# Two experts at a time: the first half of a pair's combine moves ahead of the next pair's gather

## The chip, the core and the metric

The kernel runs on one core of a Trainium2 chip. The core has a matrix engine (TensorE; PE in the profile, PEld where it loads weights), VectorE (DVE), ScalarE (ACT), GpSimd (POOL) and SyncE (SP), which here issues the weight transfers. Each engine works through its own list of instructions in order and waits at semaphores for the others. Matrix products land in PSUM, which this kernel uses as eight banks of 128 x 512 floats. The metric is the device time of one execution in microseconds (us), as the median of several runs.

## The reference

Two transformer blocks on 256 tokens of width 1024, in float32. The change touches the last part of the second block alone: a mixture of 32 experts (4 groups of 8, two experts per token, each with a hidden width of 512):

```
y = jnp.zeros_like(h)
for g in range(G):
    hg = jnp.einsum('td,edf->tef', h, w_gate[g])
    hu = jnp.einsum('td,edf->tef', h, w_up[g])
    act = jax.nn.silu(hg) * hu * comb[:, g, :, None]
    y = y + jnp.einsum('tef,efd->td', act, w_down[g])
```

`comb` is zero for every expert that the router did not choose for a token. The result is h + y.

## The kernel before

Everything ahead of the experts takes the first 555 us. Then the 32 experts are worked through as 16 pairs, p = 0 to 15, in the loop of `moe`; `step` ties each piece of TensorE's work behind the piece before it, so the order in which the loop is written is TensorE's order. An expert gets 64 slots for tokens; a pair fills the 128 rows of the array. For pair p the pieces are:

- `select`: VectorE builds a one-hot matrix `Pm` (token to slot); it does so one pair ahead.
- `gate_up` (L1544): the gate product and the up product, each 1024 deep, in 64 matmuls of 512 columns; the two experts stand side by side in the array. Weights come from HBM in tiles of 1 MB, two tiles per half of a product.
- `activate`: ScalarE takes silu of the gate product (L1553), VectorE multiplies it with the up product and the routing weight (L1554) into `act`.
- `cols` / `gather` (L1501): the tokens of pair p + 1 are gathered by 32 small matmuls into four banks; ScalarE copies each bank into `xg` (L1503).
- `turn_act` (L1560): four transposes of `act`; ScalarE copies them into `aT` (L1562).
- `weigh` (L1513): two small matmuls for the routing weights of pair p + 1, and some short VectorE work from L1515 on.
- `down` (L1571): the down product of pair p, into two banks `py[0]` and `py[1]`, the two halves of the output's 1024 columns.
- `back` (L1529): transposes `Pm` into `PTm`, which takes slots back to tokens.
- `parts`: splits one bank of `py` into a rounded high part `yH` (ScalarE, L124) and the remainder `yL` (VectorE, L125).
- `combine(pair, n)` (L1601): takes half n of `py` back to the tokens by four matmuls (two with `yH`, two with `yL`); VectorE adds the two result banks to `acc` (L1604). If the half has not been split yet, `combine` calls `parts` itself.

A pair's combine is done while the next pair is worked on: in iteration p the loop runs `parts` and `combine` of pair p - 1. The last pair has no successor; it splits and combines its own halves within `down` (the function `halves`).

Weights: 12 tiles of 1 MB per pair. They go through 23 buffers used in turn, and SyncE issues a transfer when its buffer has been read (L1366; the last pair's down weights in eight transfers of 512 KB, L1359). Each transfer also waits until the one eight before it has landed.

Buffers that the change touches: `act`, `aT` and `yH` share two buffers in turn (tag "act"); `yL`, `xg` and `PTm` have one each. Banks are given out by the scheduler from the eight.

Of the kernel before, what the change touches and what calls it, by code (L numbers as in the profile page):

```python
# [103 lines left out]
class Builder:  # L104
# [1528 lines left out]
    def moe(self):  # L1633
        nc, tc, I, big, tmp, c = self.nc, self.tc, self.I, self.big, self.tmp, self.c
        h3 = self.h3
        fg = self.v("ffn_norm_g_2")
        self.hg = big.tile([128, KD, S], F32, name="hg", tag="acc")
        nc.vector.tensor_mul(self.hg, h3, fg[:, :, None].to_broadcast([128, KD, S]))
        self.route()
        acc = self.acc  # L1640
        self.moe_pools += ([(self.wpool, "w")] * NW + [(self.spool, "s")] * NS + [(self.npool, "n")] * NN +
                           [(self.keep, "xT")])
        self.prefetch(NW + NS + NN + 1)

        np_ = NE // 2
        pairs = {}

        def select(p):

            u = tmp.tile([128, 2, 2], F32, name="ug")  # L1650
            nc.vector.tensor_scalar_add(u, self.u, float(-128 * p - 1))
            P = tmp.tile([128, 2, 128], F32R, name="Pm")
            self.onehot(P, u, 128)
            pairs[p] = {"P": P}

        at = [None]

        def step(f, *a):

            with ExitStack() as st:  # L1660
                if at[0]:
                    st.enter_context(tc.issue_after(at[0].ins))
                at[0] = f(*a)

        def cols(p):
            pairs[p]["xg"], last = self.gather(pairs[p]["P"])
            return last

        out = self.out.rearrange("o (t p) d -> (o p) t d", p=128)

        def store(t, n):
            nc.sync.dma_start(out[:, t, 512 * n:512 * n + 512], acc[:, t, 512 * n:512 * n + 512])
        select(0)
        step(cols, 0)
        self.route_rest()
        for p in range(np_):
            q, last = pairs[p], p == np_ - 1
            load = lambda j, nm, hf: self.expert_w(2 * p + j, nm, hf)
            if not last:
                select(p + 1)  # L1680
            step(self.gate_up, q, load)
            if p == 0:
                step(self.weigh, q, 0)
            self.activate(q)
            if p:
                self.parts(pairs[p - 1], 0)
            if not last:
                step(cols, p + 1)
            if p:
                step(self.combine, pairs[p - 1], 0)  # L1690
            step(self.turn_act, q)
            if not last:
                step(self.weigh, pairs[p + 1], 2 * p + 2)
            if p:
                step(self.combine, pairs.pop(p - 1), 1)
            step(self.back, q)
            if last:
                def halves(n, i, mm):
                    at[0] = mm
                    if n and i == 0:  # L1700
                        step(self.combine, q, 0, store)
                    if i:
                        self.parts(q, n)
                step(self.down, q, load, halves)
                step(self.combine, q, 1, store)
            else:
                step(self.down, q, load)
        self.more_rounds(store)

    def more_rounds(self, store):  # L1710
# [50 lines left out]
```

## Time and profile before

| what | value |
|---|---|
| median of 3 runs | 1024.68 us (1023.98 to 1024.88) |
| the profiled execution | 1024.59 us |
| its span, first to last instruction | 1022.8 us |
| PE busy | 978.9 us, 96% of the span |
| DVE, ACT, POOL busy | 515.2, 368.8, 27.1 us |
| weight transfers of the experts (gate, up, down) | 64, 64 and 60 of 1024 KB, 8 of 512 KB |

All times below are microseconds from the start of the span. A matmul's end in the profile is modelled, and matmuls overlap: the next one starts before the one ahead of it ends. The time that a piece of TensorE's work costs is therefore read from start to start. In the chain of waits, each piece is put from the end of the one before it to its own end.

### The profile page before, as it was taken

The numbers are of one execution on the slowest core, as the hardware profiler recorded it, in microseconds if no ns is written. First come the engines' busy times: TensorE is split into PE (matmuls) and PEld (weight loads), VectorE is DVE, ScalarE is ACT, GpSimd is POOL, SyncE is SP. The second block draws the span as 40 slices with busy tenths as digits, with TensorE's granted clock in tenths as the row PEclk, the third lists the DMA queues.
The fourth block names the chain that finished last, engine by engine and source line by source line (L and its number), as shares of the span: only waits on it lengthen the run. The fifth ranks groups of instructions, "written<-read, shape, count | busy, mean of one in ns | idle before, by whom it ended". The sixth has DMA issues, their size and how long they took to land.

```text
span 1022.8 us, 16189 instructions
## 1 busy us (share of the span) xinstructions
PE 978.9 (96%) x6676; PEld 707.6 (69%) x6676; DVE 515.2 (50%) x1004; ACT 368.8 (36%) x652; POOL 27.1 (3%) x25
## 2 busy tenths in 40 slices
PE   6999999999999999999998999999999999999996
PEld 5899998999999999988995444443444444443442
DVE  4868999668866775649954122112222222112223
ACT  3555565637556453556654111110111111111110
POOL 1010000010000000230000000000000000000000
PEclk9999999999999999999999999999999999999999
DMA  9978887539955546264568999999999999999961
GB/s 315 341 282 283 284 288 279 180 124 336 327 185 180 200 163 228 69 209 137 170 241 324 369 424 420 423 421 419 425 419 424 417 425 419 421 423 420 424 251 43
DMA packets 113350, 310.20 MB, mean 303 GB/s; under 512 B 9554, under 2 KB 59128, under 8 KB 96888
## 3 DMA queue, kind: packets, MB, share of 16 engines
q1 hardware_dynamic: 113182, 309.09, 79.6%
q8 instruction: 54, 0.88, 0.3%
q14 instruction: 24, 0.20, 0.1%
q10 hardware_dynamic: 90, 0.03, 0.0%
HBM read 308.05 MB, written 1.05 MB: 302 GB/s over the span
## 4 chain that ended last, share of the span: by engine, by line
PE 92%; ACT 3%; DVE 2%; DMA 1%; issue 1%; POOL 0%; SPq 0%; DVEq 0%; ACTq 0%; POOLq 0%
PE bank L1544 21%; PE bank L129 13%; PE bank L130 13%; PE bank L131 13%; PE bank L1571 11%; PE bank L1501 6%; PE bank L1601 4%; ACT aT L1562 1%; PE g L129 1%; ACT yH L124 1%; PE g L130 1%; PE g L131 1%; PE bank L1560 1%; ACT wh L124 1%; PE bank L970 1%; PE bank L961 1%
## 5 line engine op out<-in xcount | busy, mean ns | idle before, releaser
L1544 PE MATMUL bank<-we,xg 128*64 128x512 f32 x1024 | 222.5, 592 | 0.0
L1544 PEld LDWEIGHTS bank<-we,xg 128*64 128x64 f32 x1024 | 73.5, 137 | 145.7 <-issue 144.4
L125 DVE TENSOR_TENSOR yL<-bank,yH 128x512 fp32r<-128x512 f32 x32 | 22.1, 692 | 193.5 <-ACT yH L124 193.5
L1571 PE MATMUL bank<-we,aT 128*64 128x512 f32 x512 | 113.6, 595 | 0.3 <-ACT aT L1562 0.3
L129 PE MATMUL bank<-fH,wh 128*128 128x256 f32 x352 | 100.1, 285 | 2.1 <-ACT fH L997 2.1
L130 PE MATMUL bank<-fL,wh 128*128 128x256 f32 x352 | 100.4, 285 | 0.0
L131 PE MATMUL bank<-fH,wl 128*128 128x256 f32 x352 | 100.2, 285 | 0.0
L1553 ACT ACTIVATE act<-bank 128x512 f32<-128x512 f32 x16 | 9.6, 597 | 237.7 <-PE bank L1544 237.7
L1571 PEld LDWEIGHTS bank<-we,aT 128*64 128x64 f32 x512 | 35.3, 137 | 65.3 <-issue 63.5
L1604 DVE TENSOR_TENSOR acc<-acc,bank 128x512 f32<-128x512 f32 x64 | 41.1, 683 | 61.4 <-PE bank L1601 61.3
L1503 ACT COPY xg<-bank 128x256 f32<-128x256 f32 x64 | 23.9, 373 | 129.7 <-PE bank L1501 129.7
L129 PEld LDWEIGHTS bank<-fH,wh 128*128 128x128 f32 x352 | 68.2, 194 | 2.5 <-ACT fH L997 2.5
L131 PEld LDWEIGHTS bank<-fH,wl 128*128 128x128 f32 x352 | 68.3, 194 | 0.0
L130 PEld LDWEIGHTS bank<-fL,wh 128*128 128x128 f32 x352 | 68.3, 194 | 0.0
L1501 PEld LDWEIGHTS bank<-Pm,hn 128*128 128x128 f32 x512 | 59.4, 195 | 11.5 <-issue 11.5
L1501 PE MATMUL bank<-Pm,hn 128*128 128x128 f32 x512 | 62.4, 281 | 0.0
L125 DVE TENSOR_TENSOR wl<-wup,wh 128x2048 fp32r<-128x2048 f32 x22 | 50.2, 2288 | 10.6 <-ACT wh L124 10.6
L1554 DVE SCALAR_TENSOR_TENSOR act<-bank,comb,act 128x512 f32<-128x512 f32 x16 | 12.0, 750 | 76.1 <-PE bank L1544 76.0
L130 PE MATMUL bank<-aL,wh 128*128 128x256 f32 x176 | 49.5, 283 | 0.0
L131 PE MATMUL bank<-aH,wl 128*128 128x256 f32 x176 | 49.5, 283 | 0.0
L129 PE MATMUL bank<-aH,wh 128*128 128x256 f32 x176 | 48.8, 283 | 0.0
L124 ACT CAST wh<-wup 128x2048 fp32r<-128x2048 f32 x22 | 41.8, 1902 | 14.0 <-PE bank L130 13.3
(449 smaller groups left out, 2136.9 us busy)
## 6 DMA issues: line engine op xcount, KB each, us to landing
we<-in_w_exp_gate SPq DMA_DIRECT2D x64, 1024.0 KB
we<-in_w_exp_up SPq DMA_DIRECT2D x64, 1024.0 KB
we<-in_w_exp_down SPq DMA_DIRECT2D x60, 1024.0 KB
wup<-in_w_up SPq DMA_DIRECT2D x22, 1024.0 KB
wa<-in_w_ada SPq DMA_DIRECT2D x16, 1024.0 KB
wdn<-in_w_down SPq DMA_DIRECT2D x11, 1024.0 KB
wa<-in_w_ada SPq DMA_DIRECT2D x16, 512.0 KB
wgt<-in_w_in SPq DMA_DIRECT2D x8, 1024.0 KB
```

Source lines behind the costliest of these rows:

```text
L124: self.hi = self.nc.scalar.copy(hi, raw)
L125: self.nc.vector.tensor_sub(lo, raw, hi)
L129: mm(o, lh, rh, start=start, stop=False, skip_group_check=True)
L130: mm(o, lh, rl, start=False, stop=False, skip_group_check=True)
L131: return mm(o, ll, rh, start=False, stop=stop, skip_group_check=True)
L1501: last = nc.tensor.matmul(b[:, i], self.hn[:, t, cc + i], P[:, t].bitcast(F32), start=(t == 0), stop=(t == 1), skip_group_check=True)
L1503: nc.scalar.copy(xg[:, cc:cc + 2], b)
L1544: last = mm(b[64 * j:64 * j + 64], pair["xg"][:, kk, 64 * j:64 * j + 64], w[j][:, k], start=(kk == 0), stop=(kk == 7), skip_group_check=True)
L1554: nc.vector.scalar_tensor_tensor(act, pu, pair["comb"], act, op0=OP.mult, op1=OP.mult)
L1571: return self.nc.tensor.matmul(py[n][64 * j:64 * j + 64], aT[:, ff, 64 * j:64 * j + 64], w, start=(ff == 0), stop=(ff == 3), skip_group_ch ...
L1601: last = nc.tensor.matmul(bs[t], PT[:, t], y, start=(i == 0), stop=(i == 1))
L1604: nc.vector.tensor_add(o, o, bs[t])
```

## The change

The first half of pair p - 1 (`py[0]`) is now split at the end of iteration p - 1, directly behind `down`, instead of behind `activate` in iteration p. Its `combine` runs directly behind the gate and up products of pair p, ahead of the gather instead of behind it. The second half (`py[1]`) is split right behind that combine, by a call of its own ahead of the gather, where before `combine(..., 1)` called it behind `turn_act` and `weigh`. Nothing is added to or taken from the computation; every instruction is there as often as before.

```diff
@@ -1683,11 +1683,10 @@
                 step(self.weigh, q, 0)
             self.activate(q)
             if p:
-                self.parts(pairs[p - 1], 0)
+                step(self.combine, pairs[p - 1], 0)
+                self.parts(pairs[p - 1], 1)
             if not last:
                 step(cols, p + 1)
-            if p:
-                step(self.combine, pairs[p - 1], 0)
             step(self.turn_act, q)
             if not last:
                 step(self.weigh, pairs[p + 1], 2 * p + 2)
@@ -1705,6 +1704,7 @@
                 step(self.combine, q, 1, store)
             else:
                 step(self.down, q, load)
+                self.parts(q, 0)
         self.more_rounds(store)
```

On TensorE, in one pair of the loop (lines that begin with - stand there before, + now):

```order
 L1571 MATMUL bank<-we,aT 64x512 x16
 L1544 MATMUL bank<-we,xg 64x512 x32
-L1501 MATMUL bank<-Pm,hn 128x128 x16
 L1601 MATMUL bank<-yH,PTm 128x512 x2
 L1601 MATMUL bank<-yL,PTm 128x512 x2
+L1501 MATMUL bank<-Pm,hn 128x128 x16
 L1560 MATMUL bank<-cst,act 128x128 x4
 L1513 MATMUL bank<-carry,Pm 128x6 x2
```

The gather and the first combine change places; the transposes of `act` and all behind them stay. (A float32 matmul is two in the profile, so 32 here is 64 there.)

On ScalarE, one pair of the kernel before, with buffer numbers (bank_6967 and bank_6968 are the two halves of one pair's down product):

```order
L1553 ACTIVATE act_7052<-bank_7002 128x512
L124 CAST yH_7055<-bank_6967 128x512
L1503 COPY xg_7059<-bank_7060 128x256
L1503 COPY xg_7059<-bank_7066 128x256
L1503 COPY xg_7059<-bank_7072 128x256
L1503 COPY xg_7059<-bank_7078 128x256
L1562 COPY aT_7097<-bank_7092 128x512
L124 CAST yH_7109<-bank_6968 128x512
```

and the same stretch now, for the pair after it (bank_7126 and bank_7127 are the two halves):

```order
L124 CAST yH_7152<-bank_7126 128x512
L1553 ACTIVATE act_7215<-bank_7165 128x512
L124 CAST yH_7226<-bank_7127 128x512
L1503 COPY xg_7230<-bank_7231 128x256
L1503 COPY xg_7230<-bank_7237 128x256
L1503 COPY xg_7230<-bank_7243 128x256
L1503 COPY xg_7230<-bank_7249 128x256
L1562 COPY aT_7101<-bank_7096 128x512
```

The split of the second half has moved from behind the copy of `aT` to ahead of the four copies of `xg`, and that of the first half from behind the silu to ahead of it. On VectorE the second `yL` (L125) moves with it: it stands directly behind the two adds of the first combine now, ahead of the short work of `weigh` (L1515 to L1518); before it stood behind that.

## Rows read from the trace of the kernel before

**Rows 1.** Chain of waits, three pairs and the end: start us, us, what.

```profile
643.69 13.73 PE bank L1544 x64
...
672.33 13.73 PE bank L1544 x64
...
987.29 13.73 PE bank L1544 x64
...
1011.76 1.89 PE bank L1571 x8
```

**Rows 2.** Timeline of TensorE: start us, us, engine line op out<-in xcount [idle before].

```profile
657.36 3.84 PE L1501 MATMUL bank<-Pm,hn 128*128 128x128 f32 x32
660.95 0.71 PE L1601 MATMUL bank<-yH,PTm 128*128 128x512 f32 x2
...
661.96 0.60 PE L1560 MATMUL bank<-cst,act 128*128 128x128 f32 x4
662.32 0.36 PE L1513 MATMUL bank<-carry,Pm 128*128 128x6 f32 x2
663.72 0.73 PE L1601 MATMUL bank<-yH,PTm 128*128 128x512 f32 x2 [1.04 <-ACT yH L124]
...
665.03 0.29 PE L1529 MATMUL bank<-identr,Pm 128*128 128x128 f32 x2
665.25 1.08 PE L1571 MATMUL bank<-we,aT 128*64 128x512 f32 x4
```

**Rows 3.** Groups by line, 574 to 1010 us: xcount | busy us, mean ns | idle.

```profile
L1513 PE MATMUL bank<-carry,Pm 128*128 128x6 f32 x32 | 5.8, 253 | 0.0
```

**Rows 4.** Waits of TensorE, 585 to 1010 us: total us, times, longest.

```profile
PE bank L1601 <- ACT yH L124: 15.8, 15, 1.2
```

**Rows 5.** Timeline of ScalarE in the same pair.

```profile
661.23 0.37 ACT L1503 COPY xg<-bank 128x256 f32<-128x256 f32 x1 [0.52 <-PE bank L1501]
662.60 0.59 ACT L1562 COPY aT<-bank 128x512 f32<-128x512 f32 x1 [0.99 <-PE bank L1560]
663.08 0.59 ACT L124 CAST yH<-bank 128x512 fp32r<-128x512 f32 x1
```

**Rows 6.** Timeline of VectorE in the same pair.

```profile
661.92 1.28 DVE L1604 TENSOR_TENSOR acc<-acc,bank 128x512 f32<-128x512 f32 x2 [3.67 <-PE bank L1601]
...
663.70 0.69 DVE L125 TENSOR_TENSOR yL<-bank,yH 128x512 fp32r<-128x512 f32 x1
```

**Rows 7.** Stretches: us, busy (x) by engine, PEclk, DMA share, GB/s.

```profile
574.00:985.00 411.00, 396.05 (x2084) 184.12 (x2084) 97.62 (x277) 53.03 (x117) 0.00 (x0) 1.00 1.02 421
985.00:991.00 6.00, 6.00 (x32) 2.00 (x30) 0.00 (x0) 0.00 (x0) 0.00 (x0) 1.00 0.51 184
```

**Rows 8.** Timeline of SyncE: the last issue of weights.

```profile
978.99 0.50 SPq L1359 DMA_DIRECT2D we<-in_w_exp_down  x1
```

**Rows 9.** Timeline of TensorE in the last pair.

```profile
1000.96 0.73 PE L1601 MATMUL bank<-yH,PTm 128*128 128x512 f32 x2
...
1003.75 0.73 PE L1601 MATMUL bank<-yH,PTm 128*128 128x512 f32 x2 [1.16 <-ACT yH L124]
...
1005.04 0.29 PE L1529 MATMUL bank<-identr,Pm 128*128 128x128 f32 x2
```

**Rows 10.** Waits of SyncE, 960 to 980 us.

```profile
SPq L1359 <- DMA we<-in_w_exp_up: 0.7, 1, 0.7
```

**Rows 11.** Timeline of VectorE in the last pair.

```profile
1001.95 1.28 DVE L1604 TENSOR_TENSOR acc<-acc,bank 128x512 f32<-128x512 f32 x2
```

**Rows 12.** Stretches, as in rows 7: two idle times and what followed.

```profile
230.00:233.00 3.00, 0.93 (x6) 0.50 (x5) 1.17 (x3) 1.82 (x5) 0.00 (x0) 1.00 0.38 68
233.00:236.00 3.00, 3.00 (x17) 3.00 (x17) 2.62 (x8) 0.99 (x3) 0.00 (x0) 0.56 1.01 396
...
438.00:441.00 3.00, 1.73 (x13) 1.44 (x12) 2.33 (x2) 2.62 (x5) 2.67 (x2) 1.00 0.03 4
441.00:444.00 3.00, 3.00 (x23) 2.78 (x22) 1.75 (x1) 0.00 (x0) 2.82 (x2) 1.00 0.95 287
```

## The prediction

> **What bounds the kernel now.** I read the page first (the table above), then the chain of waits, then the timeline of each engine through one pair, and last the stretches of the weight transfers. The chain shows the experts as one repeated pattern: the products of pair after pair start 28.64 us apart (643.69 to 672.33), and it stays on TensorE almost throughout [rows 1]. The timeline of TensorE shows the one hole in a pair: after the two small matmuls of `weigh` it sits idle for 1.04 us until ScalarE has split the second half of the previous pair [rows 2]. It is there 15 times and costs 15.8 us [rows 4]. ScalarE's timeline says why: that split (663.08) stands behind the fourth copy of `xg` and the copy of `aT`, and `aT` waits for the transposes [rows 5]. The data have been ready since the last `down`; only the order of the list holds them back.
>
> The second bound hides behind that. From 574 to 985 us the DMA engines are full, share 1.02, and move 421 GB/s [rows 7]. A pair's weights are 12 x 1.0486 = 12.58 MB, which at that rate take 29.9 us, 1.25 more than TensorE needs for a pair. TensorE does not wait, because it lives on tiles loaded ahead, and that stock shrinks with each pair. What TensorE gains can be kept only as long as it lasts.
>
> **The change part by part.**
>
> *The wait that goes.* `weigh` has two matmuls in 0.36 us, one lasts 0.253 [rows 2, 3], so they start 0.11 apart, and a piece that waits for nothing would start at 662.32 + 0.22 = 662.54. The combine began at 663.72: 1.18 late. When nothing holds it, a combine takes 1.01 us up to the next piece (660.95 to 661.96); the second one took 1.31 (663.72 to 665.03), since `yL` also came late: another 0.30 [rows 2]. Together 1.48 us a pair. Pairs 1 to 14 have this pattern: 14 x 1.48 = 20.7 us.
>
> *What is late next.* Behind the second combine and `back`, `down` needs `aT`. The transposes start at 661.96, `aT` is copied from 662.60 to 663.19 [rows 2, 5]; `down` would start at 665.25 - 1.48 = 663.77, 0.58 later. The fourth `xg` copy now ends just ahead: it starts 0.28 after the gather's successor (661.23 against 660.95) and takes 0.37, so it leaves ScalarE 0.65 after the start of the transposes, when `aT` could start at 0.64. That cover stays, but it is the thinnest.
>
> *ScalarE.* The second `yH` now stands ahead of the `xg` copies. It needs the buffer that the first combine's `yH` matmuls read, so it runs from about 0.7 to 1.3 us after that combine starts. The first `xg` bank is ready only at about 1.9 (1.01 for the combine, and a quarter of the gather's 3.59). No collision.
>
> *VectorE.* Behind the products it has `act` and then the two adds. In the last pair, where the combine already follows the products, they start 0.99 after the combine and take 1.28 [rows 9, 11], so they end at 2.27; then `yL` (0.69, [rows 6]), done at 3.0. The second combine would start at 1.01 + 3.59 (gather, 657.36 to 660.95) + 0.36 + 0.22 = 5.2 [rows 2]. It needs `yL` and, in the built program, the bank that the second add has just read. Cover 2.2 to 2.9 us.
>
> *Moved at no cost.* A combine starts as soon behind the products as a gather does: 1000.96 against an end of 987.29 + 13.73 = 1001.02 in the last pair, 657.36 against 657.42 in another [rows 1, 2, 9]. `xg` comes 1.0 us later, but is read only behind `down`. The first half's split now stands ahead of the next silu; 13.73 us of products hide it. If one of these covers were gone, each would cost up to its length, 0.6 to 1.0 us a pair.
>
> *The weights.* SyncE's issues hang on buffers that TensorE has read. They come free earlier, which at a share of 1.02 can't raise the rate. So the weights land when they did, and the question is how early they were. At 985 us there are 6 x 184 = 1.10 MB to come [rows 7]; four tiles (4.19 MB) follow the last up tile, so that tile is in at 985 - 3.09 / 0.421 = 977.7. The last weight issue, at 978.99, waited for the landing of an up tile [rows 8, 10]: 979.0, so 1.3 us of notice come on top. Its products were due in the last quarter of `gate_up`: 987.29 + 0.75 x 13.73 = 997.6 [rows 1]. Spare: 18.6 us. One pair earlier it is 18.6 + 1.25 = 19.9, and TensorE has gained 13 x 1.48 = 19.2 by then: no wait. In pair 15 the gain of 20.7 exceeds the spare: TensorE waits about 2.1 us for up tiles, and 18.6 remain. The last down tiles are in by 991 + 1.3 and would be used at 1011.76 - 19.2 = 992.6 [rows 1, 7]: just in time.
>
> *The last pair.* There is no gather in it to cover VectorE. The adds end at 1001.95 + 1.28 = 1003.23, `yL` 0.69 later at 1003.92; before, the `yL` matmuls started 0.73 behind 1003.75, at 1004.48 [rows 6, 9, 11]. Gain 0.6. From there on, nothing changes.
>
> **Sum**, against the profiled execution (1024.59, 0.09 under the median of the runs): 18.6 + 0.6 = 19.2, so 1005.4 us. Bounds of the unknown: the spare can be read from 18.6 to 19.9 (landing at 977.7 instead of 979.0); the gain per pair from 1.04 (the idle time alone) to 1.48.
>
> **Rivals.**
>
> 1. *TensorE stays the bound to the end.* If the spare is over 20.7, all of it is kept: 20.7 + 0.6, so 1003.3. For it: the landing is inferred, not seen. Against: both readings of the spare lie below 20.7.
> 2. *`aT` takes the place of the wait.* Its cover is 0.58; if it comes 1.0 us later than I read, 0.4 us a pair stay: 14 x 1.06 + 0.6 = 15.4, below the spare, so 1009.2. For it: two copies meet on ScalarE. Against: they only touch.
> 3. *The wait for weights drops TensorE's clock.* About 2 us of idle time around 231 us were followed by a stretch at a granted 0.56, near the lower level of 1.2 GHz; 1.27 us idle around 439 were followed by 1.00 [rows 12]. Three us at 0.56 lose 1.3. My 2.1 us of waiting fall in two or three pieces with products between. If they count as one: about 1007. The Trainium skill (TensorE: Matmul & The Clock Gate, "What's actually happening") says that the throttled clock is the default and that activity releases it; the rows agree with that. By it alone a starved TensorE pays twice.
> 4. *The transfers bind already and nothing is gained.* A stage that moves 12.58 MB a pair at 421 GB/s can't run at 27.2 us a pair; with no stock it would stay where it is: 1024.6. For it: a share of 1.02 all through. Against: TensorE has 18.6 us in hand at the tightest place. The Trainium skill (DMA: Bandwidth & Descriptors, "Where 436 GB/s comes from") speaks for it: it puts the ceiling at 435 GB/s, which would be an estimated 28.9 us a pair, above the 28.64 of the trace. The trace's 421 is below that ceiling, as the rule wants.
> 5. *Slower.* VectorE's adds now decide when the second combine gets its bank. They have 2.9 us to spare; from 2.9 us late TensorE waits, from 4.4 (2.9 + 1.48) the change loses, and each us more costs 14. One us past that is 1038 or so. For it: three VectorE pieces now follow each other there. Against: they would be done 3.0 us after the combine starts, and nothing else stands among them.
>
> That the change does not do what it says is excluded by the order of the built program, in which the pieces stand as told.
>
> **Chances.** Forecast 0.62; rival 1 0.12; rival 2 0.10; rival 3 0.08; rival 4 0.05; rival 5 0.03. The range 1003.0 to 1008.5 holds the forecast and rivals 1 and 3, 0.82. A measurement of this kernel can tell 0.2%, 2 us, from no change: faster 0.92, same 0.05, slower 0.03.
>
> **What will show it.** In the changed profile, the wait of the combine for `yH` should be gone from all pairs but the very end; the products should start about 27.16 us apart from pair 2 to pair 14; the second `yH` should run before the first `xg` copy; in pair 15, and only there, TensorE should wait for up tiles, 2 us in all; the transfers should end at 988 to 991 us as before, at 421 GB/s. A period of 27.6 or more would mean a new wait in the pair (rival 2); no wait for weights at 1003, rival 1; a wait for weights in many pairs, that I read the stock too large.

## The result, and the profile after

| kernel | median us (range, runs) | profiled execution | its span |
|---|---|---|---|
| before | 1024.33 (1023.89 to 1024.88, 4) | 1024.59 | 1022.8 |
| after | 1007.44 (1005.38 to 1008.01, 4) | 1005.38 | 1003.5 |

The ratio is 0.9831, with an interval of 0.9814 to 0.9848: faster by 1.5 to 1.9%. Two repeats of the same kernel (`again` and `after_beside` below) had 1005.92 and 1006.34 us; the mean of its 14 runs is 1006.5. The forecast was 1005.4, its range 1003.0 to 1008.5.

The chain of waits first (start us, us, what). It answers to [rows 1]:

```profile
639.30 13.73 PE bank L1544 x64
...
666.46 13.73 PE bank L1544 x64
...
957.86 20.98 DMA we<-in_w_exp_up
978.88 3.65 PE bank L1544 x14
...
992.69 1.89 PE bank L1571 x8
```

The products of two pairs start 27.16 us apart instead of 28.64. Near the end, a transfer has entered the chain, which had only TensorE there before. The waits of TensorE from 555 to 1010 us (total us, times, longest), against [rows 4]:

```profile
PE bank L1544 <- DMA we<-in_w_exp_up: 2.2, 2, 1.4
PE bank L1601 <- DVE yL L125: 0.8, 1, 0.8
PE bank L1601 <- ACT yH L124: 0.7, 1, 0.7
PE bank L1571 <- ACT aT L1562: 0.3, 1, 0.3
```

The 15 waits for `yH` are gone; the one left stands at the end of the last pair, at 995 us, where before had one too (at 1014, outside the window of [rows 4]). New is a wait for up tiles. TensorE's timeline through one pair shows what stands where the wait was, against [rows 2]:

```profile
652.97 0.73 PE L1601 MATMUL bank<-yH,PTm 128*128 128x512 f32 x2
653.53 0.63 PE L1601 MATMUL bank<-yL,PTm 128*128 128x512 f32 x2
654.00 3.73 PE L1501 MATMUL bank<-Pm,hn 128*128 128x128 f32 x32
657.57 0.60 PE L1560 MATMUL bank<-cst,act 128*128 128x128 f32 x4
657.92 0.36 PE L1513 MATMUL bank<-carry,Pm 128*128 128x6 f32 x2
658.15 0.72 PE L1601 MATMUL bank<-yH,PTm 128*128 128x512 f32 x2
...
659.16 0.28 PE L1529 MATMUL bank<-identr,Pm 128*128 128x128 f32 x2
659.38 7.09 PE L1571 MATMUL bank<-we,aT 128*64 128x512 f32 x32
```

The second combine starts 0.23 us behind `weigh` and takes 1.01; nothing stands idle. ScalarE in the same pair, against [rows 5]:

```profile
653.73 0.59 ACT L124 CAST yH<-bank 128x512 fp32r<-128x512 f32 x1 [6.83 <-PE bank L1601]
655.09 0.37 ACT L1503 COPY xg<-bank 128x256 f32<-128x256 f32 x1 [0.77 <-PE bank L1501]
...
657.77 0.37 ACT L1503 COPY xg<-bank 128x256 f32<-128x256 f32 x1 [0.52 <-PE bank L1501]
658.20 0.59 ACT L1562 COPY aT<-bank 128x512 f32<-128x512 f32 x1
```

The split runs ahead of the four copies. `aT` is ready at 658.79, and `down` starts at 659.38: the thin cover of 0.6 us held. VectorE, against [rows 6]:

```profile
653.18 0.75 DVE L1554 SCALAR_TENSOR_TENSOR act<-bank,comb,act 128x512 f32<-128x512 f32 x1 [14.24 <-PE bank L1544]
653.97 1.28 DVE L1604 TENSOR_TENSOR acc<-acc,bank 128x512 f32<-128x512 f32 x2
655.17 0.68 DVE L125 TENSOR_TENSOR yL<-bank,yH 128x512 fp32r<-128x512 f32 x1
```

It is done at 655.85, 2.3 us before the second combine needs it. The last pair, on TensorE, is where the rest went (against [rows 9]):

```profile
965.13 7.89 PE L1544 MATMUL bank<-we,xg 128*64 128x512 f32 x34
973.86 3.65 PE L1544 MATMUL bank<-we,xg 128*64 128x512 f32 x16 [0.84 <-DMA we<-in_w_exp_up]
978.88 3.65 PE L1544 MATMUL bank<-we,xg 128*64 128x512 f32 x14 [1.37 <-DMA we<-in_w_exp_up]
982.46 0.73 PE L1601 MATMUL bank<-yH,PTm 128*128 128x512 f32 x2
...
985.41 0.73 PE L1601 MATMUL bank<-yL,PTm 128*128 128x512 f32 x2 [0.80 <-DVE yL L125]
...
986.19 5.37 PE L1571 MATMUL bank<-we,aT 128*64 128x512 f32 x24
...
992.62 1.94 PE L1571 MATMUL bank<-we,aT 128*64 128x512 f32 x8
```

Its products take 982.46 - 965.13 = 17.33 us. A pair that waits for nothing takes 13.84 (652.97 less the 639.13 at which this timeline starts that pair). So the weights cost 3.5 us, not the 2.2 that the waits show as idle. Matmul ends are modelled, so the beginning of a gap counts as busy. And around the gaps matmuls of the two experts, which otherwise start 0.01 us apart, run one by one: the last one ahead of the first gap starts alone at 972.42, the last two of the products at 981.51 and 981.94. The last row shows the end of it: the last `down` tiles are used at 992.62, and nothing waits for them.

The transfers run as before (stretches, columns as in [rows 7]):

```profile
574.00:985.00 411.00, 408.06 (x2155) 190.65 (x2154) 101.43 (x276) 58.26 (x121) 0.00 (x0) 1.00 1.02 420
```

One part of the difference between the two profiled executions is not the change's. The first products start at 560.3 us in the profile of before and at 558.8 in that of after. The same two stretches as in [rows 12], in after:

```profile
230.00:233.00 3.00, 0.93 (x7) 0.57 (x5) 1.36 (x3) 1.80 (x4) 0.00 (x0) 1.00 0.46 104
233.00:236.00 3.00, 3.00 (x26) 3.00 (x26) 2.73 (x8) 0.98 (x3) 0.00 (x0) 1.00 1.04 397
```

The idle time at 231 us is the same, but it was not followed by a stretch at 0.56. Ahead of it before was already 0.3 us behind, from the first 25 us; the stretch cost the other 1.1. So from here on runs are also compared by their *expert stage*: from the first of the products to the end of the span. It is 1022.8 - 560.3 = 462.5 us before and 1003.5 - 558.8 = 444.7 after.

The stage has a scatter of its own. VectorE's last add is followed only by the last store of `out`, and from that add to the end of the span it is 5.7 us in this trace of after, 6.3 and 6.5 in its two repeats, 6.0 before. So a difference of less than 0.8 us between two stages says nothing, and the sharper measure is *to the last add*: from the first product to the end of VectorE's last add. Its rows on VectorE, before and after:

```profile
1015.57 1.28 DVE L1604 TENSOR_TENSOR acc<-acc,bank 128x512 f32<-128x512 f32 x2 [0.59 <-PE bank L1601]
```

```profile
996.50 1.28 DVE L1604 TENSOR_TENSOR acc<-acc,bank 128x512 f32<-128x512 f32 x2 [0.59 <-PE bank L1601]
```

That is 456.6 us before (1015.57 + 1.28 - 560.27) and 439.0 after (996.50 + 1.28 - 558.82); the two repeats have 438.9 both. Of the 19.2 us between the profiled executions 17.6 are the change's, 1.4 the clock's ahead of the experts and 0.2 the last store's.

### The profile page after: what moved, and what is told of

It is laid out like the page before. It is cut to its first block, busy times and chain, and to the rows that moved or that the text cites. A ratio compares the mean times of both kernels' runs of the same rounds, so it can differ in the third digit from the quotient of the medians.

```text
span 1003.5 us, 16244 instructions
## 1 busy us (share of the span) xinstructions
PE 972.0 (97%) x6676; PEld 707.6 (71%) x6676; DVE 516.6 (51%) x1004; ACT 371.7 (37%) x652; POOL 27.1 (3%) x25
## 4 chain that ended last, share of the span: by engine, by line
PE 89%; DMA 3%; DVE 3%; ACT 2%; issue 1%; SPq 1%; POOL 0%; DVEq 0%; ACTq 0%; POOLq 0%
PE bank L1544 21%; PE bank L129 13%; PE bank L131 13%; PE bank L130 13%; PE bank L1571 11%; PE bank L1501 6%; PE bank L1601 3%; DMA we<-in_w_exp_up 2%; ACT wh L124 1%; DVE wl L125 1%; DMA wa<-in_w_ada 1%; PE g L130 1%; PE g L131 1%; PE bank L970 1%; PE bank L961 1%
## 5 line engine op out<-in xcount | busy, mean ns | idle before, releaser
L124 ACT CAST yH<-bank 128x512 fp32r<-128x512 f32 x32 | 18.7, 586 | 204.6 <-PE bank L1601 105.7
L1501 PE MATMUL bank<-Pm,hn 128*128 128x128 f32 x512 | 60.2, 276 | 0.0
L125 DVE TENSOR_TENSOR wl<-wup,wh 128x2048 fp32r<-128x2048 f32 x22 | 50.3, 2289 | 10.6 <-ACT wh L124 10.6
L125 DVE TENSOR_TENSOR yL<-bank,yH 128x512 fp32r<-128x512 f32 x32 | 22.0, 688 | 56.6 <-ACT yH L124 56.6
L129 PE MATMUL bank<-xH,wh 128*128 128x256 f32 x160 | 45.9, 290 | 0.6 <-ACT xH L1122 0.6
```

The costliest lines, as they stand in the source:

```text
L124: self.hi = self.nc.scalar.copy(hi, raw)
L125: self.nc.vector.tensor_sub(lo, raw, hi)
L129: mm(o, lh, rh, start=start, stop=False, skip_group_check=True)
L1501: last = nc.tensor.matmul(b[:, i], self.hn[:, t, cc + i], P[:, t].bitcast(F32), start=(t == 0), stop=(t == 1), skip_group_check=True)
```

## The experiments

Three questions: is the second half's split the whole gain; does the stock of weights cap it; and where does the capped part go. Each ratio is against the kernel before, run beside: 1024.48 us for `again` to `one_buffer_less`, 1024.82 for `second_split_late` to `fill_the_wait`, 1024.31 for the last two.

**The kernel after, again** (no edit).

> The changed kernel once more, as the base of this group. Theory 1 (the weights cap the gain): 1007.4 us as a median; TensorE waits about 2 us for up tiles in pair 15 and for nothing else in pairs 2 to 14, products 27.17 us apart. Theory 2 (no cap, the 2 us short of the forecast are spread between runs): the same time, but the wait for up tiles comes and goes. Clock: runs in which the clock falls at about 233 us, as in the profile of the kernel before, should be 1.4 us longer than runs in which it does not, whatever the experts do.

1005.92 us (1005.52 to 1006.89), ratio 0.9819 (0.9806 to 0.9833). That is 1.5 us under the 1007.4 that I expected. The wait for up tiles is 2.1 us (2.1 in `after_beside` too), so it does not come and go. The stage is 1004.1 - 558.8 = 445.3, to the last add 438.9. The first result holds.

**Fewer weights, after.** Eight tiles fewer to bring: for the second half of their down product eight experts use the tile loaded just before, so the output differs.

```diff
+            if nm == "down" and hf and e % 2 and 8 <= e < 24:
+                self.enext += 1
+                self.eloaded[key] = self.elast
+                continue
...
-            self.eloaded[key] = w
+            self.eloaded[key] = self.elast = w
```

> The changed kernel with 8 of the 192 weight tiles not loaded: in pairs 4 to 11 the second expert's second half of the down product uses the first expert's tile, so the output differs. The weights then land 8 x 2.49 = 20 us earlier at the end. Theory 1: the 2.2 us of waiting for up tiles in pair 15 go, so 2.2 us faster than the changed kernel as it is, about 1005.2 as a median. Theory 2: no difference.

1003.76 us (1002.82 to 1004.46), ratio 0.9797 (0.9784 to 0.9811). No wait for weights is left. TensorE's timeline in the last pair:

```profile
966.73 13.90 PE L1548 MATMUL bank<-we,xg 128*64 128x512 f32 x64
980.56 0.73 PE L1605 MATMUL bank<-yH,PTm 128*128 128x512 f32 x2
```

The products take 13.83 us again, 3.5 less than after. By the median it gains 2.2 us over `again`, as expected; but the first products of this execution came 1.6 us later than those of `again`, so the median hides a part. By the stage (1001.6 - 560.4 = 441.2) it is 4.1, of which 0.6 is the last store; to the last add, 438.9 - 435.5 = 3.4. The cap is real, and without it the change would be worth 456.6 - 435.5 = 21.1 us.

**Fewer weights, before.** The same edit on the kernel before.

> The kernel before with the same 8 tiles not loaded. Both theories: TensorE never waited for weights there, so 1024.3 us, no change. Together with the run before it this gives what the change is worth where weights are no limit: theory 1 says 14 x 1.47 + 0.5 = 21.1 minus nothing, so about 19.1 to 21.1 us.

1024.97 us, ratio 1.0003 (0.9994 to 1.0012), with the old wait still there (view of waits, 585 to 1010 us):

```profile
PE bank L1605 <- ACT yH L124: 15.8, 15, 1.2
```

To the last add it is 456.6 us, as before. So weights cost nothing there: the same bytes are a bound only once TensorE is faster.

**One buffer less, after.**

```diff
-        self.moe_pools += (... + [(self.npool, "n")] * NN + [(self.keep, "xT")])
-        self.prefetch(NW + NS + NN + 1)
+        self.moe_pools += (... + [(self.npool, "n")] * NN)
+        self.prefetch(NW + NS + NN)
```

> The changed kernel with 22 weight buffers in place of 23 (the last of the list is left out), nothing else. Theory 1: the transfers stop for full buffers around 561 us one tile earlier, so every later tile lands 2.49 us later, and the wait for up tiles in pair 15 (or one before it) grows from 2.2 to 4.7 us: 2.5 us slower than the changed kernel, about 1009.9. Theory 2: no difference, since 22 buffers still run far ahead of TensorE.

1009.97 us (1009.2 to 1010.22), ratio 0.9855 (0.984 to 0.987): 4.05 over `again` where 2.5 was expected. The stage is 1008.5 - 560.2 = 448.3, 3.0 over `again` (3.0 to the last add, too); the first products came 1.3 us later than those of `again`. The waits:

```profile
PE bank L1544 <- DMA we<-in_w_exp_up: 3.7, 3, 1.3
...
PE bank L1544 <- DMA we<-in_w_exp_gate: 0.2, 1, 0.2
```

A tile of 1.0486 MB is 2.5 us at 421 GB/s, and that less in stock costs 3.0. The wait now reaches back into pair 14.

**Second split late.** The kernel after without one line:

```diff
                 step(self.combine, pairs[p - 1], 0)
-                self.parts(pairs[p - 1], 1)
```

> The kernel after without its line that issues the second split beside the gather: the second combine again splits its own half, behind the ScalarE copy of aT, as before; the first combine stays ahead of the gather. Theory 1 (the gain is the wait for the second half's yH, which the early second split takes away): the wait of about 1.2 us for yH is back in front of the second combine in all 15 pairs, the period of a pair is 28.6 us again, the time 1024 us (1022.5 to 1025.5). Theory 2 (a part of the gain comes from the first combine's place directly behind the up products): period 27.4 to 28.3 us, time 1008 to 1019 us.

1024.61 us (1022.1 to 1025.16), ratio 0.9997 (0.9988 to 1.0007). The wait is back as it was (view of waits):

```profile
PE bank L1601 <- ACT yH L124: 15.8, 15, 1.2
```

Products start 28.62 us apart (642.86 to 671.48 in the chain). In this kernel the whole gain hangs on this line; moving the first combine alone gains nothing.

**Only the splits moved.** The kernel before with both splits ahead of the gather, in buffers of their own, and one weight buffer less; TensorE's order stays.

```diff
-NW, NM, NS, NT, NR, NX, NN = 3, 2, 4, 2, 7, 5, 3
+NW, NM, NS, NT, NR, NX, NN = 3, 2, 4, 2, 7, 5, 2
...
-        yH = self.tmp.tile([128, 512], F32R, name="yH", tag="act")
-        yL = self.tmp.tile([128, 512], F32R, name="yL", bufs=1)
+        yH = self.tmp.tile([128, 512], F32R, name="yH", tag="yH")
+        yL = self.tmp.tile([128, 512], F32R, name="yL")
...
             if p:
                 self.parts(pairs[p - 1], 0)
+                self.parts(pairs[p - 1], 1)
             if not last:
                 step(cols, p + 1)
```

> TensorE's order of the kernel before (gather, then both combines), but both splits issued ahead of the gather, in buffers of their own (two for yH, two for yL), paid for with one weight buffer less (22 instead of 23). Theory 1 (what counts is that the second split is ready, not where the first combine stands): no wait for yH or yL in front of the second combine, period about 27.2 us, time as the run with one buffer less: 1010 us (1008 to 1012.5). Theory 2 (the first combine has to cover the split's time): a wait of 0.5 us or more in each pair stays, in front of either combine or of the down products, period 27.7 us or more, time 1015 to 1024 us.

1008.2 us (1007.92 to 1009.11), ratio 0.9838 (0.9823 to 0.9853). TensorE's timeline in a pair:

```profile
654.60 3.84 PE L1501 MATMUL bank<-Pm,hn 128*128 128x128 f32 x32
658.19 0.71 PE L1601 MATMUL bank<-yH,PTm 128*128 128x512 f32 x2
...
659.56 0.36 PE L1513 MATMUL bank<-carry,Pm 128*128 128x6 f32 x2
659.78 0.72 PE L1601 MATMUL bank<-yH,PTm 128*128 128x512 f32 x2
...
661.02 7.09 PE L1571 MATMUL bank<-we,aT 128*64 128x512 f32 x32
```

No hole, 27.17 us a pair (640.94 to 668.11 in the chain). So the first combine need not stand ahead of the gather as such. What its place buys in the change is memory: the second `yH` takes over the buffer that the first combine has just read. Here the buffers of the splits were paid for with a weight buffer (whether there is room without that was not tried), and the time is near that of the run with one buffer less. It is 1.4 us better by the stage (446.9 against 448.3), 1.5 to the last add. Of this 1.1 are the last pair's, from the first combine to `down` (2.62 us against 3.73): the wait for `yL` is gone there.

**First split late.**

```diff
+                self.parts(pairs[p - 1], 0)
                 step(self.combine, pairs[p - 1], 0)
...
-                self.parts(q, 0)
```

> The kernel after, but the first half's split is issued behind the next pair's activation, directly ahead of the first combine, not at the end of its own pair. Theory 1 (the gain rests on the second split alone): ScalarE and VectorE are done with it before TensorE comes to the first combine or at most 0.2 us behind, period 27.2 to 27.4 us, time 1005.5 to 1008.5 us. Theory 2 (the first split's early place is needed too): a wait for yH or yL of 0.5 us or more in front of the first combine in each pair, period 27.7 us or more, time 1013 us or more.

1007.01 us, ratio 0.9826 (0.9811 to 0.9841); same waits as after, stage 1005.4 - 560.0 = 445.4, to the last add 438.8, products 27.17 us apart (640.52 to 667.69). The change's third edit, the first split at the end of its own pair, does nothing for the time.

**Fill the wait.** In the last pair both combines go into the products, where TensorE waits for weights.

```diff
+                if between and nm == "up":
+                    between(hf, last)
...
-            step(self.gate_up, q, load)
+            if last:
+                def between(n, mm):
+                    at[0] = mm
+                    step(self.combine, pairs[p - 1], n)
+                    if n == 0:
+                        self.parts(pairs[p - 1], 1)
+                step(self.gate_up, q, load, between)
...
-            if p:
+            if p and not last:
                 step(self.combine, pairs[p - 1], 0)
...
```

> The kernel after, but in the last pair the two combines of the pair before stand inside the products: the first between gate and up, the second between the two halves of the up product, where TensorE waits for the last weights. Theory 1 (what is left of the uncapped gain, about 2.2 us, is TensorE's wait for the last up tiles, and only that): the wait shrinks by the 1.0 us or so of combine work that now stands in it, so 0.7 to 1.7 us faster than the kernel after in the same call: 1004.3 to 1005.3 us beside 1005.9. Theory 2 (the last weight's landing sets the end whatever TensorE does before): the combine's time is given back by a longer wait, the time does not move by more than 0.3 us.

1005.27 us (1004.35 to 1005.53), ratio 0.9806 (0.9793 to 0.982). TensorE's timeline in the last pair:

```profile
966.23 7.44 PE L1546 MATMUL bank<-we,xg 128*64 128x512 f32 x32
...
979.70 4.00 PE L1546 MATMUL bank<-we,xg 128*64 128x512 f32 x16
984.62 0.66 PE L1562 MATMUL bank<-cst,act 128*128 128x128 f32 x4 [0.91 <-DVE act L1556]
...
985.95 5.37 PE L1573 MATMUL bank<-we,aT 128*64 128x512 f32 x24 [0.55 <-ACT aT L1564]
```

From the first product to `down` it is 985.95 - 966.23 = 19.72 us, against 986.19 - 965.13 = 21.06 after: 1.3 us. The wait for weights is gone, but 0.91 and 0.55 us came up for `act` and `aT`, which the combines had covered in their old place. The last up matmuls start 979.70 - 559.92 = 419.8 us after the first product, 420.1 after, so hardly earlier; what is won is that the combines no longer stand behind them. The stage is 1003.5 - 559.9 = 443.6. The median is 0.65 us under that of `again`, just less than what the first theory wanted, and the intervals overlap. So both kernels ran once more beside each other.

> The kernel after, unchanged, beside the run that fills the wait, so that the two share a call: 1005.4 to 1008 us, TensorE's wait for the last up tiles 2.1 us.

> The kernel that fills the wait in the last pair, once more, beside the kernel after. Theory 1 (the wait for the last weights is TensorE's, work put into it is won, less what the two combines covered in their old places): from the first product of the expert stage to the span's end 1.1 to 1.7 us less than the kernel after, as in the first pair of profiles (443.6 beside 445.3), and the median of the times 0.7 to 1.7 us lower. Theory 2 (the 0.65 us between the medians of the first two calls was the scatter of single executions): medians within 0.3 us, the stage within 0.5 us.

After: 1006.34 us (1005.51 to 1007.73), ratio 0.9827 (0.9812 to 0.9841), stage 1005.8 - 560.4 = 445.4. With the wait filled: 1006.21 (1004.24 to 1007.2), ratio 0.9824 (0.9808 to 0.984), stage 1003.3 - 559.8 = 443.5. The medians do not show the gain that I expected: they are 0.13 us apart. By the stage it is 1.9 us here and 1.7 against `again`, but a part of both is the last store. The last add of the first run that fills the wait:

```profile
996.27 1.28 DVE L1606 TENSOR_TENSOR acc<-acc,bank 128x512 f32<-128x512 f32 x2 [0.59 <-PE bank L1603]
```

To the last add it is 437.6 there and 437.7 in the second, against 439.0, 438.9 and 438.9 in the three of after: 1.2 us, each time. Over all runs the means of the times are 1005.5 (10 runs) and 1006.5 (14), 1.1 us apart with an uncertainty of 0.8. So the gain is seen in the traces, and at the edge of what the times can tell.

Why the times scatter can be seen in the three profiles of the unchanged kernel after: to the last add 439.0, 438.9 and 438.9, but first products at 558.8, 558.8 and 560.4, and the last store 5.7, 6.3 and 6.5. The late one of the first products has a lower clock in the first 20 us. This stretch in after and in `after_beside`:

```profile
12.00:20.00 8.00, 5.82 (x32) 5.15 (x32) 4.21 (x7) 3.05 (x3) 0.00 (x0) 0.79 1.11 344
```

```profile
12.00:20.00 8.00, 5.91 (x28) 4.71 (x25) 3.30 (x7) 3.61 (x4) 0.00 (x0) 0.64 1.11 344
```

## Why the prediction was right

*The wait that goes: right.* 28.64 to 27.16 us a pair is 1.48, the figure predicted, and `second_split_late` takes it away again. For pairs 1 to 14 I had 20.7 us. From the first product to the first of the last pair it is 987.12 - 560.27 = 426.85 before and 965.13 - 558.82 = 406.31 after: 20.5.

*What is late next, ScalarE, VectorE: right.* The second `yH` starts 0.76 us after the first combine (0.7 predicted), VectorE has 2.3 us in hand (2.2 to 2.9), `aT` 0.59 (0.58).

*The weights: right in kind, mis-sized.* I put the spare at 18.6 us, so that 20.7 - 18.6 = 2.1 would be lost in pair 15, and there alone. The loss is there and only there, but it is 3.5, so the spare was 20.5 - 3.5 = 17.0. This is the term of the sum that was mis-sized. That the waits view shows 2.2 is a coincidence of two different counts. `fewer_after` gives the 3.5 back. The landing itself came when I said: the second wait ends at 978.88, and I had 979.0. But the stage began 1.4 us earlier than in the profile I worked from, and the landing did not come 1.4 us earlier with it: the last up tile is in 420.1 us after the first product, where it had been 979.0 - 560.3 = 418.7. In `again` and `after_beside` it is 420.0 too, also with the late start, while the last weight issue of `second_split_late` stands at 418.9, near before; so this goes with the shorter pairs. The transfers as a whole do not run later: counted from the first product, 306.2 MB have moved by 420 us in the trace before and in that of after, and the last weights are in at 430.3 in both (990.55 and 989.15 us of the span, within the 988 to 991 that I had put down). The delay enters at one step: SyncE's issues follow each other every 2.4 to 2.6 us, until in after one interval, from 404.0 to 407.8, is 3.8; before goes on at 2.4 there (403.9 to 406.3 to 408.7). Why one tile is noticed 1.3 us later, at the same rate, stays open.

*The last pair: right, slightly large.* The second combine starts `yL` at 985.41 in the last pair; from the first combine to the start of `down` it is 986.19 - 982.46 = 3.73 us. Before it was 5.26 - 0.96 = 4.30 (`down` stands 0.22 behind the 1005.04 of [rows 9]). Gain 0.57 where I had 0.6; what is left of VectorE's wait is 0.8.

*The sum.* 20.5 - 3.5 + 0.6 = 17.6, the measured difference to the last add, against a forecast of 19.2. The profiled execution hit 1005.4 by luck: the 1.4 us that the cap took more were given by the clock ahead of the experts. The typical run, at 1006.5, shows the change's own worth.

*The rivals.* 1 (TensorE the bound to the end) did not happen, but its 21.3 us are nearly what `fewer_after` shows (21.1). 2 (`aT`): no wait in any pair but the first. 3 (clock): the granted clock (the column ahead of the DMA share) stayed at 1.00, the upper level of 2.4 GHz, through the gaps for weights. Stretches of after:

```profile
975.00:978.00 3.00, 2.51 (x12) 0.69 (x8) 0.00 (x0) 0.00 (x0) 0.00 (x0) 1.00 1.00 386
978.00:981.00 3.00, 2.12 (x10) 0.77 (x12) 0.00 (x0) 0.00 (x0) 0.00 (x0) 1.00 1.04 386
```

4 (transfers bind, nothing gained): wrong as a whole, since the stock carries 14 pairs; right for the last 3.5 us. The transfers of after moved 420 GB/s, as those of before did within 1. The Trainium skill (DMA: Bandwidth & Descriptors, "Where 436 GB/s comes from") puts the ceiling of the fabric at 435 GB/s, and the trace stays under it again; it also has the HBM side bind such transfers at about 358, which this trace, at 420, does not bear out. 5 (slower by VectorE's adds): its cover of 2.3 us was never used up.

## What to carry to other kernels

An engine that works through its list in order waits for the place of an instruction, not for its data: moving one split ahead of four copies was worth 1.48 us a pair, and the combine that moved with it only made its buffer free in time. Where a stage moves more bytes than its rate allows and lives on a stock, work out at which step the stock runs out before you count a gain per step; what goes beyond it is lost at that step alone. Price a wait from start to start of the work around it, since the idle time in the view of waits was 2.2 us of 3.5 lost.

## What the runs showed of the hardware

- The weight transfers slowed near the end at an unchanged share: in the two stretches above, 386 GB/s at 1.00 and 1.04, against 420 at 1.02 over the stage. The last pair's `down` tiles come then, in halves of 512 KB. That the halves are the cause was not tried.
- The same idle time at 231 us was followed by a granted clock of 0.56 in the profile of before and of 1.00 in that of after, with the same code there (a mean of the two levels, 1.2 and 2.4 GHz, against the upper one). It cost 1.1 us, less than the 1.3 to 1.4 that I had put on it: the first matmul behind the idle time starts at 232.73 before and 232.43 after, 0.30 apart, and the one behind the wait near 439 us at 440.04 and 438.67, 1.37 apart.
- The last store of `out`, from VectorE's last add to the end of the span, took 5.7 to 6.5 us over twelve traces, and 5.7, 6.3 and 6.5 in three of the same kernel. What sets it was not tried.
